# One-operation modulation row sums spread over later stages, and rotary tables built on a 128x128 tile, in a fused attention, short-convolution and FFN block

## Chip, cores and metric

The kernel runs on one NeuronCore of a Trainium2 chip. The metric is the device time of one execution in microseconds (us); the time of a kernel is the median of its runs. The engines are TensorE (PE: matrix products and transposes), VectorE (DVE), ScalarE (ACT), GpSimd (POOL) and SyncE (SP), which issues the DMAs. Each engine works through its own instructions in order.

## The reference

One transformer block on one sequence of S = 1024 tokens, width D = 1024, fp32:

```
s_a, g_a, gate_a, s_f, g_f, gate_f = six rows of (silu(c) @ w_ada + b_ada)   # 6 x 1024
h    = LN(x) * (1 + scale) + shift
proj = h @ w_in          # 256 c_q, 128 c_kv, 32 rotary key, 3 x 512 conv
q    = rms(c_q) @ w_q_up ; k, v = rms(c_kv) @ w_kv_up       # 8 heads, 64 + 32
rotary on 32 dims: ang = position * theta^(-2i/32), cos and sin (16 angles)
y_attn = attention, causal by chunks of 64
y_conv = gate_b * causal_dwconv3(gate_c * conv_v)
x1 = LN(alpha * x + gate_a * (group_rms([y_attn, y_conv]) @ w_out))
h2 = LN(x1) * (1 + scale_f) + shift_f
u  = causal_dwconv3(h2 @ w_up) ; f = (silu(u_g) * u_v) @ w_down         # 2816 wide
out = LN(alpha * x1 + gate_f * f)
```

What the change touches is the first line (each of the 6 x 1024 modulation values is a dot product of silu(c) with a row of 1024 weights) and the cos and sin tables.

## The kernel before, in words

Matrix products run as three matmuls each, on operands split into a high and a low fp32r half: ACT casts the high half (L136, or DVE at L138) and POOL or DVE subtracts it for the low half (L139). The stages follow one another, and a tile scheduler orders the instructions of each engine outside the FFN; inside the FFN pairs a table written by hand does.

- **Modulation, LN and input projection.** For each of 8 blocks j of 128 features `mod_col` (L277) makes two columns of `modm`, each by `row_dots` (L263): two multiply-and-sum operations on 128x512 (L271, with an accumulator read each), an add of the halves (L274) and the bias (L279, L281). `make_h` (L284) transposes xn on PE (`tpa`, L288), ACT scales and shifts (`hf`, L289), the result is split into `hTh`, `hTl`, and `mm3_w` (L292) multiplies by w_in (`pa`, L296, for c_q and c_kv).
- **rms and rotary key.** `rms_apply` (L166) norms c_q and c_kv (`rq0`, `rk0`: squares on ACT, row sums on PE, L182), with a float32 split on DVE (L138). PE makes the rotary key (`psr`, L426). DVE reduces the angles position times frequency, modulo two pi, on 128x1024 tiles `cosT`, `sinT` that hold the same 16 frequencies eight times (L373 to L394); two Sin activations on ACT end it (L395, L396).
- **Conv branch.** Four slices i of three parts of 48 matmuls (`psc`, L296) through two PSUM tiles; weights are loaded, cast on ACT (`hwc`) and split on POOL (`lwc`, L139). ACT and DVE evict (L535, L537), take the three taps (L508, L511), and DVE multiplies by the gate (L541). Between them stand the query and key projections (`psqr`, `psk`, `psq`), the rotation (`rope`, L402 to L413, with row swaps by DMA) and **32 dots of the four other modulation rows** (`ada_rest`, L496, called four times with i = 0 and 1): each loads 128x1024 weights by SP into one of two buffers (`y[:, 2 + j % 2]`, L499), and DVE dots it with silu(c) and adds the bias (L271, L274, L501).
- **Attention** (scores `s` L607, softmax, transposes `tp` L641, `o` L631).
- **Output projection.** Eight token tiles t of 48 matmuls (`pso`, L717); DVE adds the residual (L822) and takes two layer norms (L145 to L160). `h2_half` (L794) transposes x1 (`tpc`, L799) for tokens 0 to 511 after tile 3 and for the rest after tile 7, with modulation rows 1 and 2 (`modr`).
- **FFN.** A first pair, then pairs (`al`, `p`, L960) in the order of a table (`step` L1092, `ahead` L1101: i is the pair, n its step), then the down groups (`pd`, L1166). In pairs 4 to 11 `ahead` reloads x1 into `ra`, and at pair 5 spreads row 3 into `gate_f`.

Of the kernel before, what the change touches and what calls it, by code (L numbers as in the profile page):

```python
# [11 lines left out]
F32 = mybir.dt.float32  # L12
F32R = mybir.dt.float32r
AF = mybir.ActivationFunctionType
ALU = mybir.AluOpType
PSUM = bass.MemoryType.PSUM

P = 128
S = 1024
D = 1024  # L20
KD = D // P
NT = S // P
# [10 lines left out]
C_BM = 0  # L33
C_BF = 16
# [33 lines left out]
def block_kernel(ctx: ExitStack, tc: tile.TileContext, a: dict, out: bass.AP, dbg=None):  # L68
    nc = tc.nc
    V, A, G, T, SP = nc.vector, nc.scalar, nc.gpsimd, nc.tensor, nc.sync  # L70
    dbg = dbg or {}

    def dump(name, t):
        if name in dbg:
            SP.dma_start(out=dbg[name], in_=t)
# [28 lines left out]
    cp, const = pool_("const")  # L104
    cols = const.tile([P, C_N], F32, name="cols")
    kcol = const.tile([P, 2], F32, name="kcol")
# [17 lines left out]
    def col(i):  # L124
        return cols[:, i:i + 1]
# [137 lines left out]
    def row_dots(pool, tag, rows, name):  # L263

        n = len(rows)
        part = pool.tile([P, n, 2], F32, tag=tag + "p", name=name + "p", bufs=2)
        for i, r in enumerate(rows):
            for hf in range(2):
                sl = slice(hf * 512, (hf + 1) * 512)
                junk = pool.tile([P, 512], F32, tag=tag + "j", name=f"{name}j{i}{hf}")  # L270
                V.tensor_tensor_reduce(out=junk, in0=r[:, sl], in1=cact[:, sl], scale=1.0, scalar=0.0,  # L271
                                       op0=ALU.mult, op1=ALU.add, accum_out=part[:, i, hf:hf + 1])
        res = pool.tile([P, n], F32, tag=tag + "s", name=name + "s", bufs=2)
        V.tensor_tensor(res, part[:, :, 0], part[:, :, 1], op=ALU.add)  # L274
        return res

    def mod_col(j):  # L277
        acc = row_dots(xpool, "mod", [ada[j][:, 0, :], ada[j][:, 1, :]], f"mod{j}")
        V.tensor_scalar(out=modm[:, j, 0:1], in0=acc[:, 0:1], scalar1=col(C_BM + 2 * j), scalar2=1.0,  # L279
                        op0=ALU.add, op1=ALU.add)  # L280
        V.tensor_scalar(out=modm[:, j, 1:2], in0=acc[:, 1:2], scalar1=col(C_BM + 2 * j + 1), scalar2=None,  # L281
                        op0=ALU.add)
# [87 lines left out]
    posi = ta.tile([P, S], mybir.dt.int32, tag="gc", name="posi")  # L370
    SP.dma_start(out=posi, in_=a["pos"].partition_broadcast(P))
    ang = cosT
    V.tensor_copy(ang, posi)  # L373
    V.tensor_scalar(out=ang, in0=ang, scalar1=kcol[:, 0:1], scalar2=None, op0=ALU.mult)
    n1 = ta.tile([P, S], F32, tag="cu", name="n1")
    n2 = sinT
# [19 lines left out]
    A.activation(out=sinT, in_=ang, func=AF.Sin, scale=kcol[:, 1:2])  # L396
    A.activation(out=cosT, in_=n1, func=AF.Sin, scale=-1.0, bias=halfpi)
# [98 lines left out]
    def ada_rest(v):  # L496
        for j in range(KD):
            raw = y[:, 2 + j % 2, :]
            SP.dma_start(out=raw, in_=a["ada_r"][v, j])  # L499
            acc = row_dots(ta, "rest", [raw], f"rest{v}{j}")  # L500
            V.tensor_scalar(out=modr[:, v, j:j + 1], in0=acc, scalar1=col(C_BF + KD * v + j),  # L501
                            scalar2=1.0 if v == 1 else 0.0, op0=ALU.add, op1=ALU.add)
# [15 lines left out]
    for i in range(4):  # L518
# [25 lines left out]
        if i < 2:  # L544
            ada_rest(2 * i)
            ada_rest(2 * i + 1)
# [13 lines left out]
    dump("modr", modr)  # L560

# [201 lines left out]
    h2 = [[h0pool.tile([P, KD, 512], F32R, name=f"h2{nm}0") for nm in "hl"]]  # L763

# [38 lines left out]

    rt = []
    for t in range(NT):
        sl = slice(t * P, (t + 1) * P)
        xt = tc_.tile([P, D], F32, tag="x", name=f"xr{t}")
        SP.dma_start(out=xt, in_=a["x"][sl, :])
        if t == 0:
            ya = {0: y_split(0, 0)}  # L810
        if t + 1 < NT:
            ya[t + 1] = y_split(t + 1, 0)
            if t > 0:
                so[t + 1] = (None, y_split(t + 1, 1))
        ps = so[t][0]
        if t > 1:
            ps = bigtile(f"pso{t}")
            out_mm(t, ps, 1, so[t][1])
        out_mm(t, ps, 0, ya[t])
        r = tc_.tile([P, D], F32, tag="r", name=f"r{t}", bufs=5)  # L820
        rt.append(r)
        V.scalar_tensor_tensor(out=r, in0=xt, scalar=ALPHA, in1=flat(ps), op0=ALU.mult, op1=ALU.add)  # L822
        mu, rs = ln_stats(tc_, r, "lnc")
        ln_affine(r, mu, rs, g1, b1_)
        A.mul(ra[t], eight(r), ALPHA)
        SP.dma_start(out=eight(x1s[t]), in_=ra[t])
        mu, rs = ln_stats(tc_, r, "lnd")
        ln_apply_act(tc_, r, r, mu, rs, "lnd")
        if t == 3:
            h2_half(0)  # L830
# [69 lines left out]
    gate_f = h0pool.tile([P, D], F32, name="gate_f")  # L900
# [210 lines left out]
    with in_order():  # L1111
        for j, (i, n) in enumerate(order):
# [10 lines left out]
            if n == 6 and 4 <= i < 4 + NT:  # L1123
                SP.dma_start(out=ra[i - 4], in_=x1s[i - 4])
            if n == 6 and i == 5:
                gate_row(gate_f, 3, "gf", lambda name: bank("pd", name))
# [62 lines left out]
def prepare(inputs):  # L1189
# [5 lines left out]
    o["pos"] = ca(g["positions"][0])  # L1195
# [34 lines left out]
    kc = np.zeros((P, 2), np.float32)  # L1230
    kc[:, 0] = np.tile(inv, P // 16)
    kc[:, 1] = np.tile(np.repeat(np.array([-1.0, 1.0], np.float32), 16), P // 32)
# [27 lines left out]
```

## Time and profile before

| | before |
|---|---|
| median of 3 runs (lowest, highest) | 1265.99 us (1263.84, 1267.23) |
| the profiled execution's own time | 1269.46 us |
| its span in the trace | 1267.2 us |
| mean granted TensorE clock in it | 0.969 |
| busy, as a share of the span: PE, DVE, ACT, POOL | 91%, 70%, 43%, 37% |

Times in the trace count from the start of the span. An engine's busy time leaves out waits; idle time before an instruction is put down to whatever released it last. The granted clock of a stretch is the mean level at which TensorE was let run, as a share of 2.4 GHz.

### The profile page before, as it was taken

To read this page: it belongs to the slowest core of one execution; us is meant where nothing else is said; L and a number is where in the kernel's file an instruction comes from. 1 tells how busy PE (TensorE), PEld (TensorE's weight loads), DVE (VectorE), ACT (ScalarE), POOL (GpSimd) and SP (SyncE) were. 2 spreads that over 40 slices of the span, in tenths; PEclk is the share of its full clock that TensorE was granted. 3 is DMA by queue.
4 is the path that set the end of the run, shared out by engine and by line. 5 is a ranking of instruction groups with operands and counts; after the bars stand their busy time and mean duration, and the time that the engine had idled before them with its cause. 6 is when DMAs were issued, how large, how long until landed. Compare 5 with 4: busy or idle time off the path is not lost.

```text
span 1267.2 us, 14305 instructions
## 1 busy us (share of the span) xinstructions
PE 1151.6 (91%) x5204; PEld 933.0 (74%) x5204; DVE 887.2 (70%) x1293; ACT 549.0 (43%) x856; POOL 471.7 (37%) x308
## 2 busy tenths in 40 slices
PE   1898979769989889998999999999999999999996
PEld 1766757647877668876778888888888777888885
DVE  6965789876767756678967778778778694444247
ACT  2554322326767942436554544544545432221011
POOL 4656635323166832452720000000000377843126
PEclk9889989899989999999999999999999999999998
DMA  9401365653154122222122323312212444321002
GB/s 375 151 26 50 106 211 170 163 149 70 29 135 108 67 99 85 83 84 83 67 83 84 116 96 120 116 71 96 84 67 83 150 166 166 133 103 64 1 34 100
DMA packets 46218, 134.46 MB, mean 106 GB/s; under 512 B 5452, under 2 KB 15308, under 8 KB 45124
## 3 DMA queue, kind: packets, MB, share of 16 engines
q1 hardware_dynamic: 46148, 133.55, 31.7%
q8 instruction: 41, 0.67, 0.2%
q14 instruction: 29, 0.24, 0.1%
HBM read 100.76 MB, written 19.92 MB: 95 GB/s over the span
## 4 chain that ended last, share of the span: by engine, by line
PE 64%; DVE 16%; DMA 6%; POOL 5%; ACT 3%; issue 3%; SPq 1%; DVEq 0%; POOLq 0%; ACTq 0%
PE al L960 16%; PE pd L1166 14%; PE p L960 12%; PE pso L717 6%; PE s L607 3%; PE psc L296 2%; PE tp L641 2%; DMA y<-ada_r_in 2%; PE pa L296 2%; PE pu L844 1%; PE o L633 1%; PE o L631 1%; DVE cu L511 1%; POOL y L1147 1%; DMA kb1l<-plk 1%
## 5 line engine op out<-in xcount | busy, mean ns | idle before, releaser
L1089 POOL TENSOR_TENSOR wr<-wr,gate_f 128x1024 f32<-128x1024 f32 x22 | 63.4, 2890 | 351.4 <-DMA wr<-w_down_in 351.4
L1170 DVE TENSOR_TENSOR y<-pd,y 128x512 f32<-128x512 f32 x96 | 61.5, 683 | 97.9 <-PE pd L1166 97.9
L1166 PE MATMUL pd<-h2l,h2h 128*128 128x512 f32 x480 | 115.2, 390 | 0.3 <-DVE y L1170 0.2
L1166 PEld LDWEIGHTS pd<-h2l,h2h 128*128 128x128 f32 x480 | 90.1, 188 | 19.8 <-DVE y L1170 1.1
L296 PE MATMUL psc<-hTh,hwc 128*128 128x512 f32 x192 | 64.9, 405 | 13.9 <-DVE y L541 8.1
L1008 DVE SCALAR_TENSOR_TENSOR rbuf<-rbuf,cols,rbuf 128x1023 f32<-128x1023 f32 (+1 forms) x52 | 70.0, 1346 | 0.0
L645 DVE TENSOR_TENSOR ptl<-tp,pth 128x512 fp32r<-128x512 f32 (+1 forms) x96 | 50.6, 550 | 20.5 <-ACT pth L644 20.0
L296 PE MATMUL psc<-hTl,hwc 128*128 128x512 f32 x192 | 64.8, 404 | 0.0
L296 PE MATMUL psc<-hTh,lwc 128*128 128x512 f32 x192 | 64.2, 402 | 0.0
L612 DVE TENSOR_REDUCE mx<-s 128x1 f32<-128x128 f32 (+3 forms) x64 | 47.6, 752 | 18.4 <-PE s L607 16.9
L296 PEld LDWEIGHTS psc<-hTh,hwc 128*128 128x128 f32 x192 | 37.1, 195 | 24.1 <-issue 10.5
L928 DVE TENSOR_TENSOR wf<-wr,wf 128x512 fp32r<-128x512 f32 x53 | 36.4, 686 | 25.1 <-ACT wf L927 25.1
L614 ACT ACTIVATE p<-s,mx 128x128 f32<-128x128 f32 (+3 forms) x64 | 47.8, 748 | 12.7 <-DVE mx L612 12.4
L960 PE MATMUL p<-h2h,wf 128*128 128x512 f32 x160 | 53.0, 392 | 0.0
L644 ACT CAST pth<-tp 128x512 fp32r<-128x512 f32 (+1 forms) x96 | 43.7, 485 | 19.5 <-PE tp L641 17.4
L960 PE MATMUL al<-h2h,wf 128*128 128x512 f32 x160 | 51.9, 393 | 0.0
L1006 ACT ACTIVATE rbuf<-rbuf,cols 128x1024 f32<-128x1024 f32 x26 | 32.4, 1246 | 41.7 <-DVE rbuf L999 41.3
L641 PE MATMUL tp<-ident,p 128*128 128x128 f32 x288 | 48.2, 278 | 0.7 <-DVE ptl L645 0.6
L139 POOL TENSOR_TENSOR h2l<-wr,h2l 128x1024 fp32r<-128x1024 f32 x10 | 26.2, 2629 | 52.9 <-ACT h2l L136 36.8
L296 PEld LDWEIGHTS psc<-hTh,lwc 128*128 128x128 f32 x192 | 37.8, 197 | 8.3
L296 PEld LDWEIGHTS psc<-hTl,hwc 128*128 128x128 f32 x192 | 37.5, 195 | 8.1
L927 ACT CAST wf<-wr 128x512 fp32r<-128x512 f32 x58 | 35.6, 615 | 14.1 <-PE al L960 11.1
(888 smaller groups left out, 3396.3 us busy)
## 6 DMA issues: line engine op xcount, KB each, us to landing
wr<-w_up_in SPq DMA_DIRECT2D x44, 512.0 KB
y<-ada_r_in SPq DMA_DIRECT2D x32, 512.0 KB
wr<-acts SPq DMA_DIRECT2D x22, 512.0 KB
wr<-w_down_in SPq DMA_DIRECT2D x22, 512.0 KB
ada<-ada_m_in SPq DMA_DIRECT2D x8, 1024.0 KB
acts<-rbuf SPq DMA_DIRECT2D x15, 512.0 KB
rwc<-w_conv_in SPq DMA_DIRECT2D x12, 512.0 KB
xn<-x_in SPq DMA_DIRECT2D x8, 512.0 KB
```

The lines of the kernel that those rows point to most:

```text
L296: T.matmul(out=ps[hf][0:n_out, :], lhsT=w[:, k, :], rhs=hT[hf][m][:, k, :], start=first and i == 0, stop=last and i == 2)
L612: V.tensor_reduce(out=mx, in_=st[:, 0:n], op=ALU.max, axis=mybir.AxisListType.X, negate=True)
L614: A.activation(out=pt[:, 0:n], in_=st[:, 0:n], func=AF.Exp, bias=mx, accum_out=sm[:, c:c + 1])
L641: T.transpose(tp[:, q4 * P:(q4 + 1) * P], pts[q4][:, kt * P:(kt + 1) * P], ident)
L644: A.copy(pth[:, c0:], tp[:, c0:])
L645: V.tensor_tensor(ptl[:, c0:], tp[:, c0:], f(pth[:, c0:]), op=ALU.subtract)
L717: T.matmul(out=ps[:, hf, :], lhsT=l[:, i, :], rhs=r[:, hf * 512:(hf + 1) * 512], start=part == 1 and i == 0 and n == 0, stop=part == 0 and ...
L960: T.matmul(out=ps, lhsT=w[:, m, k, :], rhs=b[mb][:, k, :], start=first and k == 0 and n == 0, stop=k == 3 and n == 2, skip_group_check=True)
L1008: V.scalar_tensor_tensor(out=u[:, d:S], in0=src[:, 0:S - d], scalar=w, in1=u[:, d:S], op0=ALU.mult, op1=ALU.add)
L1089: G.tensor_tensor(raw, raw, gate_f, op=ALU.mult)
L1166: T.matmul(out=ps[hf], lhsT=l[:, sl], rhs=r[:, hf * 512:(hf + 1) * 512], start=k == 0 and m == 0, stop=k == n - 1 and m == 2)
L1170: V.tensor_tensor(rs_, ps[hf], rs_, op=ALU.add)
```

## The change

**Row sums.** `row_dot` is one multiply-and-sum over 128x1024, writing its products over the row, and one accumulator read; the halves and the add are gone. **Place of the 32 dots.** Row 0 (8 dots) stays with i = 0 of the conv branch. Rows 1 and 2 (16 dots) go to the output projection, six each for tiles 0 and 1 and four for tile 2, loaded in turn into `sinT` and `gate_f`; for these c is loaded again into `cosT` and gets its Silu there. Row 3 (8 dots) goes to FFN pairs 4 to 11, loaded at step 0 into `ra[7]` and dotted at step 6 with a third silu(c) in `ra[6]`; the x1 reload moves to pairs 6 to 13 and the gate row to pair 12. **Rotary tables.** The host repeats each block of 128 positions for 16 partitions, so that a 128x128 tile holds all 16 frequencies of all 1024 positions once; the reduction runs on it, three Sin activations make -sin, sin and cos (`trig`), eight DMAs write them to DRAM (`tab`) and twelve read them back into `sinT` and `cosT`.

```diff
-    def row_dots(pool, tag, rows, name):
...
-            for hf in range(2):
-                sl = slice(hf * 512, (hf + 1) * 512)
-                junk = pool.tile([P, 512], F32, tag=tag + "j", name=f"{name}j{i}{hf}")
-                V.tensor_tensor_reduce(out=junk, in0=r[:, sl], in1=cact[:, sl], scale=1.0, scalar=0.0,
-                                       op0=ALU.mult, op1=ALU.add, accum_out=part[:, i, hf:hf + 1])
-        res = pool.tile([P, n], F32, tag=tag + "s", name=name + "s", bufs=2)
-        V.tensor_tensor(res, part[:, :, 0], part[:, :, 1], op=ALU.add)
-        return res
+    def row_dot(pool, tag, r, ca, name):
+
+        acc = pool.tile([P, 1], F32, tag=tag, name=name, bufs=4)
+        V.tensor_tensor_reduce(out=r, in0=r, in1=ca, scale=1.0, scalar=0.0, op0=ALU.mult, op1=ALU.add, accum_out=acc)
+        return acc
...
-    posi = ta.tile([P, S], mybir.dt.int32, tag="gc", name="posi")
-    SP.dma_start(out=posi, in_=a["pos"].partition_broadcast(P))
-    ang = cosT
+    posi = ta.tile([P, P], mybir.dt.int32, name="posi")
+    SP.dma_start(out=posi, in_=a["pos"])
+    ang, n1, n2 = [ta.tile([P, P], F32, name=nm) for nm in ("ang", "n1", "n2")]
...
-    A.activation(out=sinT, in_=ang, func=AF.Sin, scale=kcol[:, 1:2])
-    A.activation(out=cosT, in_=n1, func=AF.Sin, scale=-1.0, bias=halfpi)
+    trig = ta.tile([P, 3, P], F32, name="trig")
+    for i, (src, scale, bias) in enumerate(((ang, -1.0, 0.0), (ang, 1.0, 0.0), (n1, -1.0, halfpi))):
+        A.activation(out=trig[:, i, :], in_=src, func=AF.Sin, scale=scale, bias=bias)
+
+    tab = tc.dram_tile([3, 16, S], F32, name="tab")
+    for b in range(KD):
+        SP.dma_start(out=tab[:, :, b * P:(b + 1) * P].rearrange("i r t -> r i t"), in_=trig[16 * b:16 * b + 16])
+    for b in range(4):
+        SP.dma_start(out=sinT[32 * b:32 * b + 32, :], in_=tab[0:2].rearrange("i r t -> (i r) t"))
+        for i in range(2):
+            SP.dma_start(out=cosT[32 * b + 16 * i:32 * b + 16 * i + 16, :], in_=tab[2])
...
-        if i < 2:
-            ada_rest(2 * i)
-            ada_rest(2 * i + 1)
+        if i == 0:
+            for j in range(KD):
+                ada_rest(ta, 0, j, y[:, 2 + j % 2, :], cact)
...
+    silu_c(cosT)
+    rest = [(v, j) for v in (1, 2) for j in range(KD)]
...
+        for n in range(6):
+            if rest:
+                ada_rest(tc_, *rest[0], (sinT, gate_f)[len(rest) % 2], cosT)
+                rest.pop(0)
         if t == 3:
             h2_half(0)
...
+            if 4 <= i < 4 + KD:
+                if n == 0:
+                    ada_load(3, i - 4, ra[7])
+                if n == 6:
+                    ada_dot(wupool, 3, i - 4, ra[7], ra[6])
+            if n == 6 and i >= 6 and i - 6 < NT:
+                SP.dma_start(out=ra[i - 6], in_=x1s[i - 6])
```

The scheduler moves instructions with it. Three places, with each program's own line numbers (dots are L271 before and L266 in the change; `hf` is L289 and L280; the residual is L822 and L831):

ACT in the input projection, before: `hf` of feature block 3, then that of block 4.

```order
L289 ACTIVATE hf_30_395<-tpa_396,modm 128x512
L136 CAST hTh_89<-hf_30_395 128x512
L289 ACTIVATE hf_31_404<-tpa_405,modm 128x512
L136 CAST hTh_91<-hf_31_404 128x512
L289 ACTIVATE hf_40_444<-tpa_445,modm 128x512
L289 ACTIVATE hf_41_453<-tpa_454,modm 128x512
L136 CAST hTh_89<-hf_40_444 128x512
```

The same place in the change; L388 is the three Sin activations, which read `ang` and `n`.

```order
L280 ACTIVATE hf_31_376<-tpa_377,modm 128x512
L136 CAST hTh_91<-hf_31_376 128x512
L388 ACTIVATE trig<-ang 128x128 x2
L388 ACTIVATE trig<-n_707,halfpi 128x128
L164 ACT_TABLE_LOAD
L280 ACTIVATE hf_40_409<-tpa_410,modm 128x512
```

The Sin activations and a table load now stand ahead of `hf` of block 4. What they read is written on DVE, where in the change the last part of the angle reduction (L373, L384, L385) stands around the dots of block 6 (`ada_141`); those of block 7 follow it:

```order
L272 TENSOR_SCALAR modm<-mod_445,cols 128x1
L272 TENSOR_SCALAR modm<-mod_448,cols 128x1
L373 SCALAR_TENSOR_TENSOR ang<-n_708,ang 128x128
L266 ISA ada_141,mod_487<-ada_141,y 128x1024
L266 ISA mod_487 128x1
L266 ISA ada_141,mod_490<-ada_141,y 128x1024
L266 ISA mod_490 128x1
L384 TENSOR_SCALAR ang<-ang 128x128
L272 TENSOR_SCALAR modm<-mod_487,cols 128x1
L272 TENSOR_SCALAR modm<-mod_490,cols 128x1
L385 SCALAR_TENSOR_TENSOR n_707<-ang 128x128
```

PE at the end of the input projection (`pa2b` is its last product), before: the rotary key `psr` begins after three of the four row sums `rq0p`.

```order
L296 MATMUL pa2b<-hTh_91,lwi_121 128x512
L182 MATMUL rq0p<-rq0qh_660,ones 128x512
L182 MATMUL rq0p<-rq0ql_661,ones 128x512
L182 MATMUL rq0p<-rq0qh_669,ones 128x512
L426 MATMUL psr<-hTh_89,wirs 64x512
L426 MATMUL psr<-hTh_91,wirs 64x512
```

In the change `psr` stands behind all four and behind the first row sum of c_kv as well, `rk0p`, whose operand DVE writes:

```order
L287 MATMUL pa2b<-hTh_91,lwi_121 128x512
L182 MATMUL rq0p<-rq0qh_604,ones 128x512
L182 MATMUL rq0p<-rq0ql_605,ones 128x512
L182 MATMUL rq0p<-rq0qh_613,ones 128x512
L182 MATMUL rq0p<-rq0ql_614,ones 128x512
L182 MATMUL rk0p<-rk0qh_635,ones 128x512
L425 MATMUL psr<-hTh_89,wirs 64x512
L425 MATMUL psr<-hTh_91,wirs 64x512
```

DVE in the output projection, before: what stands between the residual of tile 1 and that of tile 2.

```order
L145 BN_STATS lncst<-r_4368 128x6 x2
L147 BN_AGGR lndmv<-lndst 128x2
L708 TENSOR_TENSOR qb1l<-tpy_4395,qb1h 128x512
L147 BN_AGGR lncmv<-lncst 128x2
L155 SCALAR_TENSOR_TENSOR r_4368<-r_4368,lncmv,g_4226 128x1024
L160 SCALAR_TENSOR_TENSOR lndnb<-lndmv,lndrs 128x1
L156 SCALAR_TENSOR_TENSOR r_4368<-r_4368,lncrs,b_4227 128x1024
L145 BN_STATS lndst<-r_4368 128x6 x2
L147 BN_AGGR lndmv<-lndst 128x2
L160 SCALAR_TENSOR_TENSOR lndnb<-lndmv,lndrs 128x1
L822 SCALAR_TENSOR_TENSOR r_4453<-xr_4393,pso_4404 128x1024
```

The same place in the change, ending with the residual of tile 2:

```order
L147 BN_AGGR lncmv<-lncst 128x2
L147 BN_AGGR lndmv<-lndst 128x2
L266 ISA gate_f,rest_4070<-gate_f,cosT 128x1024
L266 ISA rest_4070 128x1
L501 TENSOR_SCALAR modr<-rest_4066,cols 128x1
L155 SCALAR_TENSOR_TENSOR r_4108<-r_4108,lncmv,g_3942 128x1024
L501 TENSOR_SCALAR modr<-rest_4070,cols 128x1
L160 SCALAR_TENSOR_TENSOR lndnb<-lndmv,lndrs 128x1
L266 ISA sinT,rest_4134<-sinT,cosT 128x1024
L266 ISA rest_4134 128x1
L156 SCALAR_TENSOR_TENSOR r_4108<-r_4108,lncrs,b_3943 128x1024
L831 SCALAR_TENSOR_TENSOR r_4217<-xr_4157,pso_4168 128x1024
```

Of the three dots there (two on `gate_f` and `sinT` in turn, and one more ahead of the first row shown) none was there before; the sixteen are spread over tiles 0 to 4 in this way, the last two of them behind the residual of tile 4.

## Rows read from the trace of the kernel before

**Rows 1.** Page, part 1: busy time and share of the span of each engine.

```profile
PE 1151.6 (91%) x5204; PEld 933.0 (74%) x5204; DVE 887.2 (70%) x1293; ACT 549.0 (43%) x856; POOL 471.7 (37%) x308
```

**Rows 2.** Stretches: length, busy time (instructions) by engine; PE clock, DMA share.

```profile
core 0: us, PE busy (x) PEld busy (x) DVE busy (x) ACT busy (x) POOL busy (x), PEclk, DMA share, GB/s
44.00:77.00 33.00, 32.74 (x160) 26.27 (x158) 22.53 (x50) 16.70 (x26) 18.38 (x12) 1.00 0.21 72
82.00:92.00 10.00, 10.00 (x35) 5.12 (x35) 9.79 (x7) 2.27 (x5) 6.72 (x4) 0.77 0.24 79
92.00:106.00 14.00, 11.10 (x49) 8.82 (x47) 12.27 (x9) 9.16 (x11) 9.96 (x6) 1.00 0.12 38
106.00:133.00 27.00, 25.46 (x102) 20.16 (x102) 11.29 (x16) 10.78 (x18) 14.90 (x11) 0.94 0.12 39
133.00:181.00 48.00, 37.17 (x160) 29.80 (x160) 42.67 (x74) 16.16 (x23) 28.37 (x17) 0.94 0.50 158
181.00:233.00 52.00, 42.31 (x162) 33.86 (x163) 45.36 (x99) 13.13 (x19) 19.40 (x11) 0.86 0.56 182
233.00:285.00 52.00, 41.09 (x169) 32.05 (x167) 37.85 (x83) 13.49 (x21) 14.93 (x11) 0.96 0.62 157
470.00:500.00 30.00, 26.87 (x114) 21.92 (x115) 17.31 (x24) 6.97 (x9) 11.30 (x14) 0.89 0.35 120
500.00:540.00 40.00, 40.00 (x196) 33.28 (x195) 26.25 (x35) 19.19 (x26) 18.14 (x21) 1.00 0.31 92
700.00:990.00 290.00, 290.00 (x1270) 238.06 (x1269) 224.04 (x286) 146.50 (x212) 2.92 (x1) 1.00 0.26 95
```

**Rows 3.** Waits of PE, 76 to 300 us: total, times, longest.

```profile
PE psc L296 <- DVE y L541: 8.1, 1, 8.1
PE psq L445 <- DVE y L541: 6.9, 1, 6.9
...
PE ry21p L182 <- DVE ry21qh L138: 3.9, 1, 3.9
```

**Rows 4.** Chain of waits, 133 to 285 us: shares by line, then pieces (start, us).

```profile
by line: DMA y<-ada_r_in 13.4%; DMA kb1l<-plk 6.8%; DVE cu L511 6.5%; DVE y L413 5.1%; DVE y L196 4.9%; issue 4.4%; DMA qb0h<-y 3.7%; SPq L492 2.3%; DVE rest30j L271 2.2%; DVE y L411 2.2%; DVE rest22j L271 2.1%; DVE gc L537 2.0%; DMA qr0sw<
...
143.29 1.98 DMA krsw<-y
186.85 4.97 DMA y<-ada_r_in
```

**Rows 5.** Timeline of DVE, 46 to 61 us: start, us, engine, line, operation.

```profile
46.85 0.68 DVE L271 CUSTOM_DVE_ANT_0 mod4j<-ada,y 128x512 f32<-128x512 f32 x1
47.46 0.08 DVE L271 DVE_READ_ACCUMULATOR2_ANT mod4p<- 128x1 f32 x1
...
58.25 1.66 DVE L271 CUSTOM_DVE_ANT_0 mod6j<-ada,y 128x512 f32<-128x512 f32 x1
...
59.95 1.13 DVE L274 TENSOR_TENSOR mod6s<-mod6p 128x2 f32<-128x2 f32 x1
```

**Rows 6.** Timeline of POOL, 53 to 61 us.

```profile
55.85 6.98 POOL L139 TENSOR_TENSOR hTl<-hf,hTh 128x512 fp32r<-128x512 f32 x4 [0.83 <-ACT hTh L136]
```

**Rows 7.** Timeline of ACT, 46 to 53 us.

```profile
47.05 0.78 ACT L289 ACTIVATE hf<-tpa,modm 128x512 f32<-128x512 f32 x1 [2.61 <-DVE modm L281]
...
52.23 0.78 ACT L289 ACTIVATE hf<-tpa,modm 128x512 f32<-128x512 f32 x1 [3.75 <-PE tpa L288]
```

**Rows 8.** Timeline of DVE, 77 to 94 us: the angle reduction on 128x1024.

```profile
81.77 5.49 DVE L383 SCALAR_TENSOR_TENSOR cosT<-n,cosT 128x1024 f32<-128x1024 f32 x2
```

**Rows 9.** Groups by line, DVE, 470 to 560 us: busy, mean ns, idle before.

```profile
L156 DVE SCALAR_TENSOR_TENSOR r<-r,lncrs,b 128x1024 f32<-128x1024 f32 x7 | 14.2, 2027 | 6.0 <-POOL lncrs L150 6.0
L155 DVE SCALAR_TENSOR_TENSOR r<-r,lncmv,g 128x1024 f32<-128x1024 f32 x7 | 9.2, 1313 | 0.2
```

**Rows 10.** Timeline of DVE, 500 to 513 us: residuals of tiles 2 and 3.

```profile
500.19 1.22 DVE L822 SCALAR_TENSOR_TENSOR r<-xr,pso 128x1024 f32<-128x1024 f32 x1
...
511.17 1.22 DVE L822 SCALAR_TENSOR_TENSOR r<-xr,pso 128x1024 f32<-128x1024 f32 x1
```

## Prediction made before the change was run

> **What bounds the kernel now.** I read the page's busy times first, then the table of stretches, and then, for the stretches in which PE is not full, its waits and the chain. PE is busy for 1151.6 of 1267.2 us and DVE for 887.2 [rows 1]: PE sets the pace, so the 32 dots on DVE cost only where DVE makes PE wait. In the pairs PE is busy for 290.00 of 290 us with DVE at 224.04, and in the input projection for 32.74 of 33 [rows 2]. The loose place is the rms and conv stretch, 82 to 285 us. Its six rows sum to 203 us, with PE busy for 167.1 and DVE for 159.2, and the granted clock falls to 0.77 to 0.96 in five of them [rows 2]. PE is thus idle for 35.9 us. A stretch at a mean clock c has lost about (1 - c) of its busy time; over the six rows that is 2.3 + 0 + 1.5 + 2.2 + 5.9 + 1.6 = 13.5 us, an estimate. With PE never waiting and its clock full, the stretch would take 203 - 35.9 - 13.5 = 153.6 us. The reader should see who holds PE: it waits 8.1 us in one wait, and 6.9 in another, for the last product of a conv slice on DVE [rows 3], and the chain of 133 to 285 us spends 13.4% on the loads of the modulation rows, ahead of every other line [rows 4]: DVE stands in order behind a dot whose weights have not landed, and the conv taps stand behind DVE.
>
> **The change, part by part.**
>
> *Conv branch: 24 of 32 dots leave, 8 get shorter.* Alone, a dot now costs two halves of 0.68, two accumulator reads of 0.08 [rows 5], the add, and a bias: some 1.8 us; beside a POOL split a half takes 1.66 and the add 1.13 [rows 5]. At 1.8 to 2.5 us each, 24 dots take 43 to 60 us of DVE's 159, and the waits for their loads go with them. DVE is left with about 110 us for a stretch of 154 and no longer sets its pace. The eight that stay keep two buffers; a load lands in up to 4.97 us [rows 4] and a dot needs about 1.6, so a pair takes about 7 us and all eight under 30, inside the conv slice they stand in. What is late next: ACT's and POOL's weight splits, the long second wait of a row sum (3.9 us, [rows 3]) and the transfer `kb1l` (6.8% of 152 us, [rows 4]). I leave 6 to 9 us of idle and clock for these, so the stretch takes some 161 us: **42 us gained**. The bounds: at best 153.6 (49 gained); at worst only the load waits go, 13.4% of 152 = 20 us.
>
> *Rotary tables.* Before, the reduction on 128x1024 stood on DVE at 77 to 95 us, with two operations at 5.49 us [rows 8]; that relief is inside the 42. On 128x128 an operation has an eighth of the elements; between the accumulator read, 0.08, and a 128x512 operation, 0.68 [rows 5], I take 0.25, nearer the small one, so 14 of them are 3.5 us. The new wait is the dear part. In ACT's order the three Sin and a table load stand ahead of `hf` of block 4, and their input is finished on DVE only after the dots of block 6. Before, ACT began block 4 at 52.23 [rows 7]. The dots of blocks 4 to 6 ran from 46.85 to 61.1 us [rows 5], partly beside the POOL splits (6.98 us for four, [rows 6]). In the change each is one operation: alone 3 x 2 x 1.3 (the price of a 128x1024 operation with two inputs, [rows 9]) = 7.8 us, stretched as before at most 14. With the 3.5 us of small operations and some 1.5 of accumulators and biases, from about 46.5, DVE finishes the angles between 59 and 65; block 1 to 3 dots end a little earlier than before, so I take 59.5. The Sin and the load add about 2, so ACT resumes at about 61.5: 9.3 us late. Behind ACT stand all later `hf` and casts, and PE, which had no gap there, runs out of blocks. I take 9.3 plus 0.7 of lower clock on its return: **10 us lost**, with bounds of 2 (DVE early, and PE holding a little work) and 15.
>
> *SP.* The 20 table transfers stand ahead of `wir` and the next weights on SP's queue, and wait for Sin at about 61.5. Small transfers landed in 1.98 us [rows 4]; writes, reads and `wir` follow one another, and `wir` lands at about 70, before `psr` wants it at 87 or later. Nothing on the path; the tables are first read by the rotation far behind.
>
> *PE's order at `psr`.* It now stands behind the first row sum of c_kv, whose split DVE writes after those of c_q. A wait of PE for such a split took 3.9 us [rows 3]. Between 0 and 5, I take **4 us lost**.
>
> *Output projection: 16 dots come.* Each is 1.3 [rows 9] + 0.08 + 0.2, or 1.6 alone, and up to 2.3 beside POOL (the mean of L156 there is 2.03, [rows 9]): 25 to 37 us. DVE is busy for 17.31 of 30 and 26.25 of 40 us [rows 2], but its chain for a tile takes 511.17 - 500.19 = 11.0 us [rows 10], as long as PE's 48 matmuls. Only its idle, 26 us over that 70, can take dots, and of it about half lies where dots stand. So DVE is 12 to 15 us late at tile 4, regains part on the tiles without dots, and PE feels it where the transposes of x1 and the seventh product tile wait for a normalized tile: **5 us lost**, bounds 0 and 14. c loaded again and its Silu on ACT lie in the last head of attention: 0, up to 3 if its load is late.
>
> *FFN pairs: 8 dots come.* A dot adds 1.6 us to a pair of 19.2 in which DVE has 66 / 290 of the time free, 4.4 us [rows 2]. PE covers it: **0.5 us lost**, bounds 0 and 3. If that cover were gone it would be 8 x 1.6 = 13.
>
> *The sum.* 42 - 10 - 4 - 5 - 0.5 = 22.5 us gained. The profiled execution took 1269.5, so such a one would take 1247.0; it stands 3.5 over the median of the runs shown, so the prediction is **1243.5 us**.
>
> **A rule weighed against the rows.** A half dot takes 0.68 us alone and 1.51 to 1.66 beside a POOL split [rows 5]. The Trainium skill, Advanced Engine Details and Errata, section VectorE Performance Modes, says that GpSimd and Vector instructions block each other where the Vector instruction is in a two-port mode, by the port that they share. By that rule alone the dots, fp32 with two inputs, might not be stretched, and the reduction would be through early (rival A); the rows speak against it here.
>
> **Rivals.**
>
> *A. ACT's wait for the angles is short.* While ACT stands, POOL gets no splits, so the dots would run alone at 1.3: 46.5 + 7.8 + 3 = 57, and less if the scheduler's earlier rows run far ahead; PE may hold two blocks of matmuls (each some 6 us) by then. 3 us lost instead of 10: 1236.5. For it: the splits end once ACT is held. Against it: six of them are still queued when DVE begins.
>
> *B. The conv branch keeps other waits.* ACT, POOL and the row swaps take the place of DVE, and of 42 us only 20 for the loads and 5 of clock are regained: 17 us less, 1260.5. For it: POOL and ACT each have weights to split in every slice; the splits' chain holds `kb1l`. Against it: at 28 of 48 and 16 of 48 us [rows 2] neither is near full.
>
> *C. The dots of the output projection run at the pace of their loads: slower.* Each dot writes over its row, so a buffer is loaded only after its dot. With two in flight the interval is (4.97 + 1.6) / 2 = 3.3 us, 53 us for sixteen, which the 55 us of tiles 0 to 4 just hold. If SP, whose queue also carries x1 and the residual's rows, keeps only one in flight, it is 6.6 us, 105 in all: 50 more, and 1243.5 - 5 + 50 = 1288. It decides the sign from (55 + 27) / 16 = 5.1 us a dot. For it: one queue in order. Against it: loads to two buffers overlapped in the conv branch.
>
> *D. The tables do not overlap.* If the 20 transfers went one after another, at 1.98 each they would end at about 102; `wir` and `psr` would be 12 us late, of which the row sums cover half: 1250. The change then does not do what it says for the rotation, since the path is longer than the one it replaces.
>
> **How the numbers follow.** Forecast 0.57, A 0.12, B 0.16, C 0.08, D 0.07. The forecast's own terms (conv 7 better to 8 worse, input projection 8 better to 5 worse, output projection 5 better to 9 worse) give 1232 to 1256 when not all go one way. Taking in A, D and B the range is **1230 to 1261**. A change of 0.3%, 3.8 us, is what a measurement can tell, so under 1262.2 is faster: forecast, A, D and most of B make 0.88; the rest of B and some bad ends 0.05 for the same; C with a little more 0.07 for slower.
>
> **What would show it.** In the trace after: the conv stretch some 40 us shorter, with no PE wait over 4 us for DVE there and a clock near 1; a gap of PE of about 9 us near 55 to 64, ended by ACT after Sin; PE's first `psr` waiting for a split of `rk0`; PE idle for a few us before tile 7 of the output projection; pairs at 19.2 us. The prediction is wrong if PE's busy share in the conv stretch stays near 0.82, or if DVE waits for loads there or in the output projection.

## The result and the profile after

The changed kernel takes 1247.8 us in the median of four runs (1245.16 to 1251.46), against 1265.95 us of the kernel before, a ratio of 0.986 with a 95% interval of 0.9829 to 0.9892: faster by 18 us. The forecast was 1243.5 with a range of 1230 to 1261. The profiled execution took 1249.48 us, its span is 1247.6; it lies 1.7 over the median, so a comparison of the two spans (19.6 us) holds within a few us.

On the page, PE is busy for as long as before [rows 1], DVE for 60 us less, in a shorter span:

```profile
PE 1153.1 (92%) x5204; PEld 931.4 (75%) x5204; DVE 827.2 (66%) x1157; ACT 547.0 (44%) x858; POOL 459.3 (37%) x308
```

To see where the time went I read, on PE's timeline, when the first or last product of each stage starts:

| PE's timeline, us | before | after | gained so far |
|---|---|---|---|
| last `pa` (input projection) | 76.6 | 82.3 | -5.7 |
| first `psr` (rotary key) | 81.8 | 92.2 | -10.4 |
| first `s` (scores) | 285.0 | 259.7 | 25.3 |
| first `pso` (output projection) | 448.3 | 420.6 | 27.7 |
| first `pu` (first pair) | 559.5 | 535.4 | 24.1 |
| first `p` (pairs) | 617.2 | 592.9 | 24.3 |
| last `p` | 1007.6 | 987.0 | 20.6 |
| end of the span | 1267.2 | 1247.6 | 19.6 |

The input projection and the row sums behind it lose 10.4, the conv branch and attention gain 38.1, the output projection gives back 3.6, the pairs 3.7 and the tail 1.0; the first pair gains 0.2.

**The loss at the start.** The stretches around the end of the input projection, then those of the conv branch, answer to [rows 2]; columns as there:

```profile
core 0: us, PE busy (x) PEld busy (x) DVE busy (x) ACT busy (x) POOL busy (x), PEclk, DMA share, GB/s
44.00:60.00 16.00, 12.14 (x59) 9.79 (x57) 15.83 (x33) 5.15 (x10) 5.10 (x4) 0.97 0.27 102
60.00:82.00 22.00, 21.23 (x94) 17.67 (x95) 0.73 (x4) 12.75 (x20) 10.17 (x8) 0.87 0.27 68
...
92.00:102.00 10.00, 9.78 (x34) 5.07 (x35) 5.75 (x4) 3.84 (x7) 8.24 (x7) 0.77 0.26 81
102.00:133.00 31.00, 29.58 (x130) 24.04 (x129) 14.67 (x16) 13.38 (x20) 19.56 (x14) 1.00 0.18 56
133.00:181.00 48.00, 44.19 (x182) 35.41 (x182) 33.22 (x47) 13.04 (x19) 26.56 (x15) 0.93 0.49 148
181.00:233.00 52.00, 50.72 (x224) 41.59 (x223) 18.35 (x21) 17.56 (x26) 24.35 (x18) 1.00 0.27 67
233.00:260.00 27.00, 25.35 (x112) 20.37 (x111) 12.49 (x17) 9.83 (x17) 8.30 (x7) 1.00 0.36 76
```

Where PE had no gap [rows 2], it now stands still for 4.63 us, up to 60.77. The timelines of ACT and PE show why: on ACT 10.69 us of waiting for the clamp of the angles (L384), the Sin, a table load, and only then `hf` of block 4, at 59.94 where it was 52.23 [rows 7]:

```profile
57.78 0.51 ACT L388 ACTIVATE trig<-ang 128x128 f32<-128x128 f32 x2 [10.69 <-DVE ang L384]
58.23 0.40 ACT L388 ACTIVATE trig<-n,halfpi 128x128 f32<-128x128 f32 x1
58.65 1.28 ACT L164 ACT_TABLE_LOAD   x1
59.94 1.45 ACT L280 ACTIVATE hf<-tpa,modm 128x512 f32<-128x512 f32 x2
60.77 1.97 PE L279 MATMUL tpa<-ident,xn 128*128 128x128 f32 x8 [4.63 <-ACT hf L280]
```

The timeline of DVE tells what the angles cost. Six of the small operations took 1.2 to 1.3 us each while POOL split (six `hTl` from 41.45 to 49.1), the others 0.2 to 0.3, and the dots of 128x1024 kept to 1.22 because POOL, fed by ACT, had run dry (last two rows):

```profile
41.49 1.32 DVE L366 TENSOR_SCALAR ang<-ang,kcol 128x128 f32<-128x128 f32 x1
42.85 1.22 DVE L369 TENSOR_SCALAR n<-ang 128x128 f32<-128x128 f32 x1
...
45.36 2.58 DVE L373 SCALAR_TENSOR_TENSOR ang<-n,ang 128x128 f32<-128x128 f32 x2
...
49.22 0.23 DVE L370 TENSOR_SCALAR n<-n 128x128 f32<-128x128 f32 x1
49.36 1.22 DVE L266 CUSTOM_DVE_ANT_0 ada<-ada,y 128x1024 f32<-128x1024 f32 x1
...
41.45 7.65 POOL L139 TENSOR_TENSOR hTl<-hf,hTh 128x512 fp32r<-128x512 f32 x6 [3.51 <-ACT hTh L136]
61.97 3.89 POOL L139 TENSOR_TENSOR hTl<-hf,hTh 128x512 fp32r<-128x512 f32 x3 [12.88 <-ACT hTh L136]
```

**The gain in the conv branch.** From the first `psr` to the first score 203.2 us became 167.5. The five rows from 92 us on sum to 159.6 of 168 us for PE and 84.5 for DVE: PE's idle fell from 35.9 to 8.4. The waits of PE between 40 and 300 us hold no conv product that waits for DVE any longer; what leads now is ACT's hold and the splits of the row sums:

```profile
PE tpa L279 <- ACT hf L280: 5.3, 2, 4.6
PE ry01p L182 <- DVE ry01qh L138: 3.8, 1, 3.8
PE rk0p L182 <- DVE rk0qh L138: 3.2, 1, 3.2
```

The 3.8 us is the old cause once more. ACT had the operand `ry01q` ready at 152.98, but its split on DVE stands behind one of the eight dots that stayed, and that dot waited 3.88 us for its load:

```profile
160.36 1.22 DVE L266 CUSTOM_DVE_ANT_0 y<-y 128x1024 f32<-128x1024 f32 x1 [3.88 <-DMA y<-ada_r_in]
...
162.23 0.42 DVE L138 CAST ry01qh<-ry01q 128x512 fp32r<-128x512 f32 x1
162.71 0.80 PE L182 MATMUL ry01p<-ry01qh,bd 128*128 128x512 f32 x1 [3.81 <-DVE ry01qh L138]
```

DVE's own waits for loads of the dots, in the conv branch (92 to 260 us) and in the output projection (420 to 536 us), in total, times, longest:

```profile
DVE y L266 <- DMA y<-ada_r_in: 8.5, 3, 3.9
DVE gate_f L266 <- DMA gate_f<-ada_r_in: 3.0, 2, 1.6
```

**The loss in the pairs.** PE's waits there, in the first pairs and the last, fell from 6.2 to 5.3 us; from 720 to 896 us PE is busy throughout in both kernels. What changed is the pitch, the time from the start of one product to the next. One block of 12 products with `tf1` takes 720.69 - 717.90 = 2.79 us in the changed kernel's timeline:

```profile
717.90 0.40 PE L972 MATMUL al<-tf1h,wf 128*128 128x512 f32 x1
718.13 0.39 PE L972 MATMUL al<-tf1l,wf 128*128 128x512 f32 x1
718.36 0.63 PE L972 MATMUL al<-tf1h,wf 128*128 128x512 f32 x2
...
720.69 0.40 PE L972 MATMUL p<-tf2h,wf 128*128 128x512 f32 x1
...
737.34 0.40 PE L972 MATMUL al<-tf1h,qb1l 128*128 128x512 f32 x1
```

and 746.13 - 743.41 = 2.72 in that of the kernel before:

```profile
743.41 0.39 PE L960 MATMUL al<-tf1h,wf 128*128 128x512 f32 x1
743.63 0.39 PE L960 MATMUL al<-tf1l,wf 128*128 128x512 f32 x1
743.86 0.61 PE L960 MATMUL al<-tf1h,wf 128*128 128x512 f32 x2
...
746.13 0.39 PE L960 MATMUL p<-tf2h,wf 128*128 128x512 f32 x1
...
762.61 0.39 PE L960 MATMUL al<-tf1h,qb1l 128*128 128x512 f32 x1
```

It is so in all 20 pairs, those without a dot too: the blocks of `tf0`, `tf1` and `tf2` have a median of 2.79 to 2.80 us, before 2.72, while those of `h2` read 2.72 (half 0) or 2.80 (half 1) in both kernels. From one block of `tf1` to that of the next pair it is 19.44 us, before 19.20.

### The profile page after: what moved, and what is told of

The parts are those of the page before. It is cut to its first block, busy times and chain, and to the rows that moved or that the text cites. A ratio compares the mean times of both kernels' runs of the same rounds, so it can differ in the third digit from the quotient of the medians.

```text
span 1247.6 us, 14202 instructions
## 1 busy us (share of the span) xinstructions
PE 1153.1 (92%) x5204; PEld 931.4 (75%) x5204; DVE 827.2 (66%) x1157; ACT 547.0 (44%) x858; POOL 459.3 (37%) x308
## 4 chain that ended last, share of the span: by engine, by line
PE 67%; DVE 13%; POOL 7%; DMA 4%; issue 4%; ACT 4%; SPq 0%; POOLq 0%; DVEq 0%; ACTq 0%
PE al L972 17%; PE pd L1189 15%; PE p L972 12%; PE psc L287 8%; PE s L613 3%; PE pso L723 2%; PE tp L647 2%; DVE ada L266 1%; PE o L639 1%; PE o L637 1%; POOL y L1170 1%; PE pa L287 1%; DVE rbuf L865 1%; DMA gate_f<-ada_r_in 1%; POOL h2l L139 1%
## 5 line engine op out<-in xcount | busy, mean ns | idle before, releaser
L1193 DVE TENSOR_TENSOR y<-pd,y 128x512 f32<-128x512 f32 x96 | 61.5, 682 | 97.6 <-PE pd L1189 97.6
L650 ACT CAST pth<-tp 128x512 fp32r<-128x512 f32 (+1 forms) x96 | 43.7, 484 | 17.8 <-PE tp L647 15.5
L279 PE MATMUL tpa<-ident,xn 128*128 128x128 f32 x64 | 12.5, 326 | 32.8 <-ACT xn L161 16.9
```

The costliest lines, as they stand in the source:

```text
L650: A.copy(pth[:, c0:], tp[:, c0:])
L1193: V.tensor_tensor(rs_, ps[hf], rs_, op=ALU.add)
```

## Experiments

Four runs of one kernel scatter by some 6 us here, and the slower ones have the lower mean clock (0.973 to 0.980 in the four of the change), so each is read by its ratio to the kernel before on the same chip and, for a part, by the starts on PE's timeline.

**1. The pairs: place in memory or traffic?** In the built program `tf0h` starts at byte 94688 of its partition before and at 94816 in the change: the four small tiles of the FFN's dots, 32 bytes each, stand ahead of it. Two runs cross the two suspects. First the change with its dots, without the tiles:

```diff
-                    ada_dot(wupool, 3, i - 4, ra[7], ra[6])
+                    m3 = modr[:, 3, i - 4:i - 3]
+                    V.tensor_tensor_reduce(out=ra[7], in0=ra[7], in1=ra[6], scale=1.0, scalar=0.0, op0=ALU.mult,
+                                           op1=ALU.add, accum_out=m3)
+                    V.tensor_scalar(out=m3, in0=m3, scalar1=col(C_BF + KD * 3 + i - 4), scalar2=0.0, op0=ALU.add,
+                                    op1=ALU.add)
```

> The changed kernel, but the eight sums of row 3 in the FFN pairs go straight into their column of modr instead of four 32-byte tiles of the weights pool. In the changed kernel the products of tf0, tf1 and tf2 have a pitch of 0.233 us where before it was 0.227, in every pair, with or without a dot in it. Theory A (place in memory): the four small tiles moved the tf tiles by 128 bytes, from 94688 to 94816; put back, the pitch is 0.227 again, pairs take 353 us from first to last p product instead of 357.5, and the median is 1243 to 1245. Rival B (traffic): the dots, their loads and what they do to DVE slow the products; the dots are still here, so the pitch stays 0.233 and the median 1248.

Measured: the blocks of `tf` take 2.72 us again (716.63 - 713.91 on PE's timeline), and first to last `p` 391.6 instead of 394.1 (the 357.5 of the expectation leaves out some 37 us at their start); 1244.53 us, ratio 0.9824 (0.9798 to 0.985), which alone would not separate it from the change (0.986).

```profile
713.91 0.39 PE L972 MATMUL al<-tf1h,wf 128*128 128x512 f32 x1
...
716.63 0.39 PE L972 MATMUL p<-tf2h,wf 128*128 128x512 f32 x1
```

Then the kernel before, without any dot in the pairs, with the place of the change:

```diff
     raws = [wupool.tile([P, 1024], F32, name=f"wr{i}", bufs=1) for i in range(2)]
+    pad = wupool.tile([P, 32], F32, name="pad", bufs=1)
+    V.memset(pad, 0.0)
```

> The kernel before with 128 unused bytes in the weights pool of the FFN, so that tf lies at 94816 as in the changed kernel; nothing else. A: the pitch of the tf products goes from 0.227 to 0.233, 3.5 to 5 us are lost, median 1269.5 to 1271. B: nothing changes, 1266.

Measured: 2.79 to 2.80 us (742.93 - 740.14), first to last `p` 393.1 instead of 390.4; 1267.71 us, ratio 1.0024 (1.0009 to 1.0039), less than expected but a loss.

```profile
740.14 0.40 PE L962 MATMUL al<-tf1h,wf 128*128 128x512 f32 x1
...
742.93 0.40 PE L962 MATMUL p<-tf2h,wf 128*128 128x512 f32 x1
```

Theory A stands: 128 bytes of place cost the pairs 2.5 to 2.7 us by these starts, and by the longer pitch alone, 0.24 us in each of 18 pairs, some 4.3 (an estimate). With the dots and their loads still there a pair takes 19.20 us again (713.91 to 733.11), so they do not show.

**2. The hold of ACT.** First with the whole reduction and the Sin at the start of the program:

```diff
     A.activation(out=cact, in_=cact, func=AF.Silu)
+    ang, n1, n2 = [y[:, 5, i * P:(i + 1) * P] for i in range(3)]
+    trig = y[:, 6, 0:3 * P].rearrange("p (i c) -> p i c", i=3)
...
```

> The changed kernel with the angles and the three Sin at the start of the program (in free slices of y), so that ACT holds no Sin ahead of hf of block 4. Theory A: ACT's wait of 10.69 us ended by the clamp of the angles is what makes the input projection end 5.75 us later than before; without it PE has no gap in that stage, psr starts 5 to 6 us earlier (at 86 to 87), median 1242 to 1243. Rival B: the row sums of c_q and c_kv and the 20 transfers on SP set when psr starts; it stays near 92, median 1247 to 1248.

Measured: 1243.67 us, ratio 0.982 (0.9787 to 0.9854), but not by the way expected. PE's gap is gone, and yet the last `pa` starts at 81.7 and `psr` at 91.3. The small operations on DVE pushed the first transposes from 15.5 to 19.1, and with the stretch at the lower clock that followed, the gain was given back (columns of the stretches as above):

```profile
44.00:56.00 12.00, 12.00 (x49) 9.96 (x49) 12.00 (x19) 6.43 (x11) 11.24 (x6) 0.77 0.39 144
56.00:77.00 21.00, 20.50 (x104) 16.57 (x103) 2.50 (x6) 11.41 (x17) 11.27 (x9) 1.00 0.22 56
```

So this run did not separate the theories. The next leaves DVE's order alone and only pins the Sin on ACT behind the copies that end the stage:

```diff
+    ended = [i for i in nc.cur_bb.bb.instructions if i.engine == mybir.EngineType.Activation][-1].name
...
         A.activation(out=trig[:, i, :], in_=src, func=AF.Sin, scale=scale, bias=bias)
+        sin_ = [q for q in nc.cur_bb.bb.instructions if q.engine == mybir.EngineType.Activation][-1]
+        tc.add_manual_dep(sin_, ended, mybir.DependencyInfo(mybir.DependencyClass.NoSync, mybir.DependencyReason.DATA),
+                          reason="late")
```

> The changed kernel with the three Sin held on ACT behind the copies that end the input projection; DVE's order stays that of the change. ACT then needs two table loads for them there. With the early Sin the wait for ACT was gone too, but the 14 small operations stood ahead of the first blocks and PE began 3.6 us later, so that run did not tell what the wait costs. Theory A: the wait of ACT sets the end of the input projection; without it PE has no gap between 44 and 77, the last pa product ends near 77 as before, psr (now behind three row sums again) starts at 84 to 87, median 1240 to 1243. Rival B: the angles on DVE between the dots are themselves the delay (the dots of blocks 4 to 7 end late); the stage ends at 81 or later and the median stays at 1246 to 1248.

Measured: the last `pa` starts at 77.5 and `psr` at 84.8, as A said: the hold costs 4.8 us, and the order of `psr`, again behind three row sums, 2.6 more. PE then waits for a row sum (second row), whose square on ACT stands behind the Sin and the two loads that they need there:

```profile
79.68 0.50 PE L182 MATMUL rq0p<-rq0qh,ones 128*128 128x512 f32 x1 [1.77 <-ACT y L346]
84.24 0.79 PE L182 MATMUL rq0p<-rq0qh,ones 128*128 128x512 f32 x1 [3.83 <-DVE rq0qh L138]
```

Of the 7.4 us, 3.8 are left at the first `pso` (416.8 against 420.6): the conv branch, now earlier, waits 2.6 for its gate product and 1.9 for another split. The ratio, 0.9826 (0.9796 to 0.9856; median 1247.18 of four runs from 1240.37), does not separate it from the change, and the median is not the 1240 to 1243 of A; the timeline, which is that of the fastest of the four, shows A's step, and that half of it is given back.

**3. Which part gains?** The change with the wide tables of before:

```diff
-    posi = ta.tile([P, P], mybir.dt.int32, name="posi")
-    SP.dma_start(out=posi, in_=a["pos"])
+    posi = ta.tile([P, S], mybir.dt.int32, tag="gc", name="posi")
+    SP.dma_start(out=posi, in_=a["pos"].partition_broadcast(P))
...
-    for i, (src, scale, bias) in enumerate(((ang, -1.0, 0.0), (ang, 1.0, 0.0), (n1, -1.0, halfpi))):
-        A.activation(out=trig[:, i, :], in_=src, func=AF.Sin, scale=scale, bias=bias)
+    A.activation(out=sinT, in_=ang, func=AF.Sin, scale=kcol[:, 1:2])
+    A.activation(out=cosT, in_=n1, func=AF.Sin, scale=-1.0, bias=halfpi)
```

> The changed kernel with the rotary tables as before (128x1024 on DVE, two Sin, no DRAM). Theory A: with 24 dots gone, DVE has room for the wide reduction in the conv branch, and the small one costs its wait on ACT: last pa at 77, psr at 82, some of that given back where rk0 and the taps stand behind the 17 us of the reduction; median 1238 to 1245. Rival B: the small reduction is worth its wait, since the wide one delays the rms norms and the first conv slice by more than 10 us: median 1249 to 1255.

Measured: 1254.37 us, ratio 0.99 (0.9877 to 0.9923): B. `psr` starts at 83.5, 8.7 earlier than in the change, but PE waits 8.5 us for the first conv slice's product on DVE, behind the wide reduction. The change with all 32 dots in the conv branch:

```diff
-        if i == 0:
-            for j in range(KD):
-                ada_rest(ta, 0, j, y[:, 2 + j % 2, :], cact)
+        if i < 2:
+            for v in (2 * i, 2 * i + 1):
+                for j in range(KD):
+                    ada_rest(ta, v, j, y[:, 2 + j % 2, :], cact)
```

> The changed kernel with all 32 dots left in the conv branch as before (two calls of 8 each with i = 0 and 1), in one operation each, tables from 128x128; none in the output projection or the pairs. Theory A: the move is what gains. The conv branch waits for DVE and the loads again, psr starts at 92 as in the changed kernel, so the gain of 36 us between psr and the first scores is mostly gone (one-operation dots keep some 10 of it), the output projection gets back 3.5 and the pairs 4: median 1258 to 1266. Rival B: the single operation and the smaller reduction freed DVE enough by themselves: median 1240 to 1250.

Measured: 1264.16 us, ratio 0.9983 (0.9966 to 1.0): A. PE waits 9.1 us for a dot's bias in one wait and 6.0 for the last gate product, as before [rows 3]. And the kernel before with `row_dot` alone (in `mod_col` too):

```diff
-            acc = row_dots(ta, "rest", [raw], f"rest{v}{j}")
+            acc = row_dot(ta, "rest", raw, cact, f"rest{v}{j}")
```

> The kernel before with the row sums in one operation and nothing else. Theory A: DVE saves some 0.3 us on each of 32 dots in the conv branch and the adds, which took up to 2.2 us beside POOL; where it stands in order behind the loads nothing is saved. 4 to 8 us: median 1258 to 1262. Rival B: the dots of the conv branch end when their loads do, and nothing is gained: 1264 to 1267.

Measured: 1254.56 us, ratio 0.9908 (0.9875 to 0.9942), 10.7 us faster, more than A said. DVE's busy time in the stretch of 82 to 285 us fell from 159.2 to 142.9:

```profile
sum 203.00, PE 171.96 PEld 134.45 DVE 142.92 ACT 68.78 POOL 103.14; mean PE 28.66 PEld 22.41 DVE 23.82 ACT 11.46 POOL 17.19
```

The prices alone give 1.8 - (1.22 + 0.08 + 0.2) = 0.3 for each of 32 dots. In that stretch the two halves and their reads took 56.0 us and the adds 12.7 before, the one operation and its read 45.2 now: 0.34 us a dot from the one operation, and 0.40 from the adds, which were stretched beside POOL as in [rows 5]. Other instructions took more, so that 16.3 of these 23.5 us are left. Together, with one-operation dots throughout, each from its own group of runs:

| median, us | 32 dots in the conv branch | 24 moved |
|---|---|---|
| wide tables | 1254.6 | 1254.4 |
| small tables | 1264.2 | 1247.8 |

Neither the move nor the small tables gain alone. With the wide tables the move saves 6.2 us between `psr` and `pso` (352.0 to 345.8) and gives them back in the output projection and the pairs; with the small ones it saves 29.9 there (358.3 to 328.4).

**4. The dots of the output projection**, left out with their loads:

```diff
-                ada_rest(tc_, *rest[0], (sinT, gate_f)[len(rest) % 2], cosT)
                 rest.pop(0)
```

> The changed kernel without the 16 dots of the output projection, their loads and the second silu(c); modulation rows 1 and 2 are set to a constant. Theory A: they cost 3.5 us (from the first pso to the first pu product 114.7 us in the changed kernel, 111.2 before): 111 again and a median of 1244 to 1245. Rival B: the loads and DVE's backlog also slow the first pairs and the end of attention: 6 us or more, 1242 or less. Rival C: they are hidden and the 3.5 us has another cause: 1248.

Measured: from the first `pso` to the first `pu` 109.9 us instead of 114.8, which is 4.9 less. Not all of that is theirs: in the first 59 us PE's clock was 0.94 and 1.00 without them, 0.91 and 0.97 with them and 0.90 and 0.98 before, so that some 1.6 us are clock (0.03 x 24.39 + 0.03 x 30, an estimate) and 3.3 are left, near the 3.6 of the first table. The median, 1248.0 of runs from 1242.59, is what C named, but too scattered to decide (ratio 0.9839, 0.9811 to 0.9868). In the change's own trace 14 of the 16 dots there stand near 1.2 us, and PE's new wait is 1.8 us at the transposes of x1 (`tpc`), which now come in one bunch.

**5. A version that beats both.** The held Sin and the sums in `modr` together:

> The held Sin of the run before and the sums of row 3 in modr, as in the run with tf at its old place, together. If both theories hold their gains add: 5 to 7 us from the start of psr, 3.5 from the pitch of the tf products: median 1236 to 1240, below both kernels.

Measured: 1237.99 us, ratio 0.9784 (0.9747 to 0.9821). Then two runs with `tf` at other places:

```diff
-    tforms = [[tfpool.tile([P, 4, 512], F32R, name=f"tf{i}{nm}") for nm in "hl"] for i in range(3)]
+    for i, nb in enumerate((32, 32, 32)):
+        V.memset(tfpool.tile([P, nb // 4], F32, name=f"pad{i}"), 0.0)
+        tforms.append([tfpool.tile([P, 4, 512], F32R, name=f"tf{i}{nm}") for nm in "hl"])
```

> The kernel with the held Sin and the sums in modr, with 32 unused bytes ahead of each of tf0, tf1 and tf2: they then start at 0, 32 and 64 modulo 256 bytes (at 224 in the kernel before and 96 in the changed one; half 1 of h2 lies at 96 in both and its products too have 0.233). Theory A: the half of a 256-byte line in which a row starts decides: below 128 slow, so all three kinds have 0.233. Theory B: starting on a multiple of 64 is what is fast: tf0 and tf2 0.227 or less, tf1 0.233.

> As the run before, with tf0, tf1 and tf2 at 128, 160 and 192 modulo 256. A: all three 0.227. B: tf0 and tf2 0.227 or less, tf1 0.233.

Measured: both theories fell. A block of 12 took 2.80, 2.76 and 2.81 us at 0, 32 and 64, and 2.80 at 128, 160 and 192; the one run of each took 1242.69 and 1247.0 us. Counted modulo 512, only 480 had given 2.72: `tf` before, and half 0 of `h2`. Half 1 lies at 352 in both kernels. The last step moves it too:

```diff
     h2.append([h2pool.tile([P, KD, 512], F32R, name=f"h2{nm}1") for nm in "hl"])
+    V.memset(h2pool.tile([P, 96], F32, name="pad"), 0.0)
```

> The kernel with the held Sin and the sums in modr, with 384 unused bytes behind half 1 of h2, so that its rows start at 480 modulo 512 bytes. Of all starts tried so far only that one (tf before, half 0 of h2) gave a pitch of 0.227; 0, 32, 64, 96, 128, 160, 192 and 352 modulo 512 gave 0.230 to 0.233, so the halves-of-a-line theory and the 64-byte theory both fell. Theory A: 480 modulo 512, which is also where every weight tile starts, is fast for any tile: the products of half 1 of h2 go from 2.80 to 2.72 us per 12, two or three blocks in each of 20 pairs, 3 to 5 us in all; median 1233 to 1236. Rival B: something else of tf and half 0 made them fast: 2.80 stays, 1238.

Measured: every kind of block in the pairs has a median of 2.72 us, half 1 of `h2` among them (743.34 - 740.62 on PE's timeline), and the kernel takes **1234.44 us, ratio 0.9742 (0.9707 to 0.9777)**, 13 less than the change. Rival B falls; why 480 is fast is another question (last section).

```profile
740.62 0.39 PE L976 MATMUL p<-h2h,wf 128*128 128x512 f32 x1
...
743.34 0.39 PE L976 MATMUL al<-h2h,wf 128*128 128x512 f32 x1
```

## Why the prediction held, and where its terms were off

- **The sum.** 22.5 us were forecast, 19.6 came between the two profiled executions and 18.2 between the medians. That this is so close is in part luck: the start lost 4.3 less than forecast for it by the last `pa`, the conv branch up to the first score gained 6.3 less, and the pairs lost 3.2 more.
- **Conv branch, 42 us.** 38.1, of which 35.7 up to the first score, the stretch that the term was made for. Mechanism and size held. Of what was left to regain, PE's idle of 8.4 us and, by the same estimate as before, 0.23 x 9.78 + 0.07 x 44.19 = 5.3 us of clock stand against the 6 to 9 that were left for both. What is late next is as named, the splits of the row sums; POOL's and ACT's weight splits are not. But behind the longest of them stands a dot's load: the eight dots took 38 us (128.34 to 166.46), not under 30, and not for nothing. So the prediction's last sign of being wrong, that DVE waits for loads in the conv branch or the output projection, did come, 8.5 and 3.0 us. It was drawn too wide, since a wait of DVE costs only what PE waits behind it: 3.8 us in the conv branch.
- **One operation and tables inside that term.** They were not priced apart. The table of run 3 shows that they could not simply be added: with either the wide reduction or the 32 dots in place, PE still waits for DVE.
- **Tables, ACT's hold, 10 us.** The place, the order and the end of the wait were right (ACT resumed at 59.94, said 61.5), but the loss was mis-sized: 5.7 at the last `pa`, of which the hold is 4.8 by run 2. ACT was 7.7 us late, and PE's gap was 4.63 us, not 9, since it still had products of the blocks before. The clock on its return, put at 0.7, cost more: 0.87 over 21.23 us of work is 2.8 by the prediction's own estimate. Inside, the stretch by POOL fell on other instructions than forecast: the small operations, put at 0.25 us, took up to 1.3, and the dots ran alone, as rival A had it.
- **The rule on shared ports.** Rival A's 1236.5 did not come, though its ground, that the dots would run alone, did: 1.22 us each. What came in their place is in DVE's rows: a 128x128 operation took 1.22 us beside POOL's splits and 0.23 after them. The rule of the Trainium skill that the prediction weighed (Advanced Engine Details and Errata, section VectorE Performance Modes), that two-port instructions and GpSimd block each other, leaves room for that with one-input operations. The two-input ones were stretched as well, 2.58 us for two. The Trainium skill's page SBUF — State Buffer, section Who interferes with whom, says that an instruction with two SBUF inputs contends with GpSimd's reads too; these rows agree with it.
- **`psr` behind the row sum of c_kv, 4 us.** 10.4 - 5.7 = 4.7 in the table; PE's wait there is the 3.2 us row for `rk0p`.
- **Output projection, 5 us.** 3.6 by the starts, some 3.3 by leaving the dots out. PE felt it where it was said, at the transposes of x1. Rival C (loads at one in flight) did not come: DVE waited 3.0 us for loads.
- **Pairs, 0.5 us.** This step failed, and its upper bound of 3 with it; the pairs take 19.44 us, not the 19.2 that were named. PE's cover was argued rightly and hides the dots, but the term looked at instructions alone. The change also allocates four tiles, and their 128 bytes moved operands of PE: 3.7 us.
- **SP and rival D.** The twenty transfers held nothing up: `psr` waited 0.4 us for `wirs`, POOL's split. They were later than said (`wir`, put as landed at 70, was issued at 76.4), but ACT casts it only at 90.4.

## What to carry to other kernels

When a helper engine sets the pace, its parts do not add: take the pair of causes away together before judging one alone. Look in the order of every engine for a late input that a moved instruction brings ahead of others; holding three small activations behind their stage was worth 7 us at its end, and half of that later (by one trace). Look also at what stands behind an instruction that waits for a load. And compare the addresses of matmul operands before and after a change, also where it only adds a tile of a few bytes.

## What was not expected of the hardware

In the pairs the pitch of a 128x512 fp32r product at the full clock depended on where the rows of the streamed operand start in a partition: 2.72 us per 12 at 480 modulo 512 bytes, 2.79 to 2.81 at 0, 64, 96, 128, 160, 192 and 352, and 2.76 at 32. The weight tiles there all start at 480 modulo 512 and were not moved, so these runs leave open whether 480 itself counts or the same place as the weights.

The down groups of the change speak against 480 itself: there both operands of these products lie in the high and the low tile of one `tf`, all at 96 modulo 512, and 12 products take 1050.19 - 1047.47 = 2.72 us:

```profile
1047.47 1.53 PE L1189 MATMUL pd<-tf2l,tf2h 128*128 128x512 f32 x6
1048.83 1.52 PE L1189 MATMUL pd<-tf0l,tf0h 128*128 128x512 f32 x6
1050.19 1.53 PE L1189 MATMUL pd<-tf1l,tf1h 128*128 128x512 f32 x6
```

The same place for both fits that. It is not the whole rule: in the two runs with `tf` at 0 to 192 the down products read 0.224 to 0.236 us in a mix, also those with both operands at 480. The cause stays open.
